# Up projection by seven products in slots, with operand splits ahead of their products, in the channel mixer of a decoder layer

## The chip, the cores and the metric

One Trainium2 chip, one core. The metric is the device time in microseconds (us) of one execution of the whole program. TensorE (PE) multiplies matrices into PSUM banks, VectorE (DVE), ScalarE (ACT) and GpSimd (POOL) work on tiles in SBUF, and SyncE (SP) issues all DMA transfers of this program on one queue.

## The reference

One layer over 2048 tokens, model width 1024, in float32. First a mixer (gated linear attention and an RWKV-7 group, chunk by chunk, with one input and one output projection), then the channel mixer, then a final norm:

```python
def conv_ffn(h, w_up, conv_w, conv_b, w_down):
    T = h.shape[1]
    u = h @ w_up
    up = jnp.pad(u, ((0, 0), (CONV_W - 1, 0), (0, 0)))
    u = sum(conv_w[j] * up[:, j:j + T] for j in range(CONV_W)) + conv_b
    gate, val = jnp.split(u, 2, axis=-1)
    return (jax.nn.silu(gate) * val) @ w_down
...
        mixed = jnp.concatenate([o_gla, o_rwkv], axis=-1) @ w_out[l]
        x = x + gt_m[:, None, :] * mixed
        h = modulate(x, norm_ffn_g[l], sh_f, sc_f)
        x = x + gt_f[:, None, :] * conv_ffn(h, ffn_up[l], ffn_conv_w[l], ffn_conv_b[l], ffn_down[l])
    return rms_norm(x, final_g)
```

The hidden width is 2816 = 22 x 128 for the gate and as much for the value.

## The kernel before

**Number format.** Every float32 operand of a large product is split into two parts, `hi` (a ScalarE cast, line 1138) and `lo` (the rest, a subtraction, line 1139), and each product is hi·hi + hi·lo + lo·hi: three matmuls of 128x512 for every 128 rows of the contraction. `split` takes VectorE or GpSimd for the subtraction by `either()` (line 1132): every third call is GpSimd's.

**First phase, to about 1431 us.** The mixer runs in 16 units over four blocks of 512 tokens. Its small matmuls leave gaps in TensorE's work; `fill()` (line 408) puts large matmuls of other work between them, `rate[0]` a step. In the last block `spare()` (line 1053), the output projection of blocks 0 to 2 (lines 276 to 278 and 445 to 447), is that filler, with `rate[0] = 0.8`, and `fill(100)` at the end issues what is left.

**Second phase, the channel mixer.** Two passes e = 0, 1 of two token blocks each (`stage_e`, line 1332). For each of 22 hidden tiles j the gate and the value of two blocks form a 2 x 2 problem that is done with seven products of half size and no eighth (a Strassen-Winograd scheme): `up_a` (line 1217) does M1 = a11·b11 and M2 = a12·b21, `up_b` (1234) M6, M7 and M5, and `up_c` (1247), a tile later, M3 and M4. The weight sums are GpSimd additions (lines 1224, 1225, 1226 and 1239). A product is 12 matmuls (lines 1212 to 1214). Banks are copied out by ScalarE (1228, 1238, 1244, 1251) and added by VectorE (1230, 1245, 1253). `conv` (1255) is the width-3 convolution: three small GpSimd copies for the halo (1257 to 1259), then per half an ACT activation and two VectorE operations (1263 to 1265). `hidden` (1269) is the gate: tanh, two VectorE operations, and the split of the result into `hh` and `hl` (1276 to 1281). Issue order per j: M1(j), M2(j), M3(j-1), M4(j-1), M6(j), M7(j), M5(j). When a group of hidden tiles is complete (2, then five times 4), `down_group` (line 1321) does its part of the down projection: 16 products of 3 matmuls per hidden tile (lines 1295 to 1297); each reads an accumulator tile `acc` from memory (1328), adds to it (1298) and writes it back (1330).

**Around it.** Before the first pass, `operands_a` and `operands_b` (1141, 1156) normalise the mixer's output and make the seven right-hand operands: I call this the entry. Between the passes (the transition) the output projection of block 3 (`stage_d`), the last down group and the operands of the second pass run together. After it the final norm (`finish`) ends the program.

**Who sets the order.** The program is written in the order above; a scheduler then sets each engine's order by priority (the place in the written order) and estimated times. Each engine, and SP's DMA queue, then works strictly in its order. Tiles come from rings: 8 for raw weights `w_st`, 4 for `w_hi`/`w_lo`, 6 for `ub`, 5 for `acc`, 6 PSUM banks. The tiles of the second phase lie where first-phase tiles lay, and one waits until what lay there is done with.

## Time and profile before

| | |
|---|---|
| median of 3 runs | 3055.96 us (3048.3 to 3060.26) |
| profiled execution, time / span | 3042.04 us / 3040.1 us |
| mean granted TensorE clock | 0.951 |
| busy share PE / DVE / ACT / POOL | 91% / 70% / 46% / 36% |
| DMA, mean over the span | 132 GB/s, hardware queue 42.0% of 16 engines |

The profile is of one execution. Times in it count from the start of its span. A row of the timeline gives the start, the duration, the engine, line and operation, and in brackets how long the engine was idle before it and what released it. A PE row's duration (0.39 us for a 128x512 matmul) overlaps its neighbours: the spacing of the starts is what a matmul costs. PEclk is the share of the full TensorE clock that was granted (1.00 is 2.4 GHz, 0.50 is 1.2 GHz).

### The profile page before, as it was taken

Reading aid. Unit: us, or ns where it says so; the run is one execution under the profiler, and the core shown is the slowest. Engines: PE = TensorE matmul, PEld = TensorE weight load, DVE = VectorE, ACT = ScalarE, POOL = GpSimd, SP = SyncE. Lnnn points to the kernel's source line nnn. Section 1 sums busy time; section 2 is a strip of 40 time slices with the busy share of each in tenths; the row PEclk is TensorE's granted clock in tenths of the full one; section 3 lists DMA queues with packets and bytes.
Section 4 is the critical chain, followed back from the end, with each engine's and each line's share of the span. In section 5 each row is a group of like instructions: output and inputs, shape, how many; then the busy total and the mean of one; then the engine's idle time right before and its main releaser. Section 6 shows DMA issues by size and latency. Waiting matters only on the chain. (4 is left out here: it accounts for less than half of the span.)

```text
span 3040.1 us, 54742 instructions
## 1 busy us (share of the span) xinstructions
PE 2776.1 (91%) x20296; PEld 2236.6 (74%) x20296; DVE 2136.3 (70%) x4248; ACT 1402.1 (46%) x2909; POOL 1102.1 (36%) x1193
## 2 busy tenths in 40 slices
PE   6998989999999999998599998989998998999997
PEld 5777777777787777777477777877776777877777
DVE  7368787877776778986877566574869756484766
ACT  4554445455554565554444334342544434342443
POOL 4223233323232224443534334252355424243441
PEclk9999998999999998999699999999998999999999
DMA  7555444443433344534142332424464442524332
GB/s 274 174 170 180 147 129 154 144 131 111 138 95 106 107 136 128 159 115 139 57 160 94 114 120 85 151 70 147 145 209 151 165 126 80 156 70 139 101 125 90
DMA packets 316875, 401.95 MB, mean 132 GB/s; under 512 B 75584, under 2 KB 148544, under 8 KB 316608
## 3 DMA queue, kind: packets, MB, share of 16 engines
q1 hardware_dynamic: 316608, 398.45, 42.0%
q8 instruction: 160, 2.62, 0.3%
q14 instruction: 107, 0.88, 0.1%
HBM read 293.49 MB, written 104.86 MB: 131 GB/s over the span
## 5 line engine op out<-in xcount | busy, mean ns | idle before, releaser
L1212 PE MATMUL g_bank<-h_hi,w_hi 128*128 128x512 f32 x1232 | 500.2, 408 | 66.9 <-ACT ub L1244 36.0
L1214 PE MATMUL g_bank<-h_hi,w_lo 128*128 128x512 f32 x1232 | 491.4, 404 | 46.4 <-POOL w_lo L1139 37.6
L1213 PE MATMUL g_bank<-h_lo,w_hi 128*128 128x512 f32 x1232 | 495.7, 402 | 7.5 <-DVE h_lo L1139 4.7
L1138 ACT CAST w_hi<-w_st 128x512 fp32r<-128x512 f32 (+1 forms) x396 | 241.0, 609 | 522.6 <-PE g_bank L1296 292.2
L1139 POOL TENSOR_TENSOR w_lo<-w_st,w_hi 128x512 fp32r<-128x512 f32 (+1 forms) x132 | 193.5, 1466 | 416.0 <-ACT w_hi L1138 376.0
L1212 PEld LDWEIGHTS g_bank<-h_hi,w_hi 128*128 128x128 f32 x1232 | 240.2, 195 | 132.3 <-ACT ub L1244 45.8
L1214 PEld LDWEIGHTS g_bank<-h_hi,w_lo 128*128 128x128 f32 x1232 | 239.8, 195 | 107.9 <-POOL w_lo L1139 41.7
L276 PE MATMUL g_bank<-h_hi,w_hi 128*128 128x512 f32 x736 | 297.5, 405 | 4.2 <-ACT carry L333 3.7
L1298 DVE SCALAR_TENSOR_TENSOR acc<-g_bank,mod,acc 128x512 f32<-128x512 f32 (+1 forms) x200 | 143.7, 727 | 217.8 <-PE g_bank L1297 179.9
L278 PE MATMUL g_bank<-h_hi,w_lo 128*128 128x512 f32 x736 | 296.0, 403 | 0.0
L277 PE MATMUL g_bank<-h_lo,w_hi 128*128 128x512 f32 x736 | 294.9, 401 | 0.0
L1213 PEld LDWEIGHTS g_bank<-h_lo,w_hi 128*128 128x128 f32 x1232 | 240.4, 195 | 62.1 <-DVE h_lo L1139 6.3
L1139 DVE TENSOR_TENSOR w_lo<-w_st,w_hi 128x512 fp32r<-128x512 f32 (+1 forms) x264 | 198.3, 752 | 83.3 <-ACT w_hi L1138 83.0
L1295 PE MATMUL g_bank<-hh,w_hi 128*128 128x512 f32 x640 | 247.2, 391 | 8.2 <-DVE acc L1298 5.3
L1296 PE MATMUL g_bank<-hl,w_hi 128*128 128x512 f32 x640 | 249.4, 392 | 1.2 <-DVE hl L1281 1.2
L1297 PE MATMUL g_bank<-hh,w_lo 128*128 128x512 f32 x640 | 247.5, 392 | 0.0
L179 ACT CAST w_hi<-w_st 128x512 fp32r<-128x512 f32 x272 | 167.5, 618 | 125.6 <-PE g_bank L277 75.5
L182 POOL TENSOR_TENSOR w_lo<-w_st,w_hi 128x512 fp32r<-128x512 f32 x90 | 125.8, 1398 | 265.4 <-ACT w_hi L179 215.8
L182 DVE TENSOR_TENSOR w_lo<-w_st,w_hi 128x512 fp32r<-128x512 f32 x182 | 139.9, 769 | 75.7 <-ACT w_hi L179 64.1
L276 PEld LDWEIGHTS g_bank<-h_hi,w_hi 128*128 128x128 f32 x736 | 140.5, 191 | 36.6 <-ACT carry L333 4.7
L278 PEld LDWEIGHTS g_bank<-h_hi,w_lo 128*128 128x128 f32 x736 | 140.9, 191 | 30.2 <-issue 0.2
L277 PEld LDWEIGHTS g_bank<-h_lo,w_hi 128*128 128x128 f32 x736 | 140.9, 191 | 28.6 <-issue 0.3
(348 smaller groups left out, 6248.9 us busy)
## 6 DMA issues: line engine op xcount, KB each, us to landing
acc<-acc SPq DMA_DIRECT2D x352, 256.0 KB, 3.1
w_st<-in_ffn_up SPq DMA_DIRECT2D x176, 256.0 KB, 2.7
w_st<-in_w_in SPq DMA_DIRECT2D x168, 256.0 KB, 3.0
proj<-ev SPq DMA_DIRECT2D x100, 256.0 KB, 3.0
w_st<-in_ffn_down SPq DMA_DIRECT2D x80, 256.0 KB, 2.7
w_st<-in_ada_t SPq DMA_DIRECT2D x64, 256.0 KB, 3.4
w_st<-in_w_out SPq DMA_DIRECT2D x64, 256.0 KB, 3.1
x_k<-in_x SPq DMA_DIRECT2D x48, 256.0 KB, 3.5
```

Of the source, the lines that this page charges most:

```text
L182: eng.tensor_tensor(out=lo[:, 0:w], in0=t[:, 0:w], in1=hi[:, 0:w].bitcast(F32), op=ALU.subtract)
L276: PE.matmul(out=ps, lhsT=wh, rhs=hi, start=k == 0, stop=False)
L277: PE.matmul(out=ps, lhsT=wh, rhs=lo, start=False, stop=False)
L278: PE.matmul(out=ps, lhsT=wl, rhs=hi, start=False, stop=k == KT - 1)
L1138: A.copy(out=hi, in_=t)
L1139: either().tensor_tensor(out=lo, in0=t, in1=hi.bitcast(F32), op=ALU.subtract)
L1212: PE.matmul(out=ps, lhsT=wh[:, c], rhs=hi, start=first and k == 0, stop=False, skip_group_check=True)
L1213: PE.matmul(out=ps, lhsT=wh[:, c], rhs=lo, start=False, stop=False, skip_group_check=True)
L1214: PE.matmul(out=ps, lhsT=wl[:, c], rhs=hi, start=False, stop=last and k == 3, skip_group_check=True)
L1295: PE.matmul(out=ps, lhsT=wh, rhs=hh, start=j == 0, stop=False)
L1296: PE.matmul(out=ps, lhsT=wh, rhs=hl, start=False, stop=False)
L1297: PE.matmul(out=ps, lhsT=wl, rhs=hh, start=False, stop=j == n - 1)
```

## The change

The up projection is written as a list of slots, one product each (`Up`, `Down`, `Other`), which `run` goes through: weights are loaded six slots ahead of their product (`load`, with the weight sums of M6), and split three slots ahead (`prep`). After each slot one piece of background work is written (`bg_step`): half a convolution, half a gate, one piece of the next operands, or, where there is none, a piece of the final norm. M3 and M4 of a tile now stand on both sides of M6 of the next, and a down group stands two products later: after M2 of the tile two behind its last one. In `parts_of` the `lo` subtraction alternates between VectorE and GpSimd for the up products and is VectorE's for all of `down`; over the program 22 of these subtractions move from VectorE to GpSimd. In the transition the output projection of block 3 is written ahead of the last down group, and the operands as background pieces. Rings: 9 `w_st` instead of 8; `ub` and the spread norms move to a pool of their own that is laid out last, the t1 operands too to one of their own; the scratch of the sums of squares shares the ring of `th`. Last, `rate[0]` in the mixer's last block is 0.55 instead of 0.8. The total number of instructions stays as it was. The core of the diff:

```diff
                 lag[0] = 2000
-                rate[0] = 0.8
+                rate[0] = 0.55
...
-    pools["np"], pools["nst"], pools["nhl"], pools["nev"], pools["nx"] = 2, 8, 4, 6, 5
+    pools["np"], pools["nst"], pools["nhl"], pools["nev"], pools["nx"] = 2, 9, 4, NX, NX
...
-        pl = h2p if name in ("b22", "t4") else h1p
+        pl = h2p if name in ("b22", "t4") else h0p if name == "t1" else h1p
...
-        return ap.tile([P, NB + 2], F32, name="ub", tag="ub", bufs=6)
+        return up.tile([P, NB + 2], F32, name="ub", tag="ub", bufs=6)
...
-    def parts_of(t, n=NB):
+    wturn = [0]
+    def parts_of(t, n=NB, down=False):
         pair = [pools["w"].tile([P, NB], F32R, name=f"w_{s_}", tag=f"w{s_}", bufs=pools["nhl"])[:, 0:n] for s_ in ("hi", "lo")]
-        split(t, pair)
+        wturn[0] += 1
+        split(t, pair, V if down or wturn[0] % 2 else G)
         return pair
...
+    bg, idle = [], []
+    def bg_step():
+        if bg:
+            bg.pop(0)()
+        elif idle:
+            idle.pop(0)()
...
+        def load(self):
+            u, j = self.u, self.j
+            half = lambda t, c: ffn_up[t][:, c * NB:(c + 1) * NB]
+            if self.what == 1:
+                u["a11"], u["a21"] = raw(half(j, 0)), raw(half(NH + j, 0))
+            elif self.what == 2:
+                u["a12"], u["a22"] = raw(half(j, 1)), raw(half(NH + j, 1))
+            elif self.what == 6:
+                u["s1"], u["s2"] = raw(), raw()
+                G.tensor_tensor(out=u["s1"], in0=u["a21"], in1=u["a22"], op=ALU.add)
+                G.tensor_tensor(out=u["s2"], in0=u["s1"], in1=u["a11"], op=ALU.add)
+                G.tensor_tensor(out=u["a21"], in0=u["a21"], in1=u["a11"], op=ALU.add)
+        def prep(self):
+            u = self.u
+            if self.what == 3:
+                G.tensor_tensor(out=u["s2"], in0=u["s2"], in1=u["a12"], op=ALU.add)
+            self.w = parts_of(u[{1: "a11", 2: "a12", 3: "s2", 4: "a22", 5: "s1", 6: "s2", 7: "a21"}[self.what]])
...
+        def post(self):
+            u, j = self.u, self.j
+            if self.what in (1, 3, 5, 6):
+                n_ = {1: "c11", 6: "c21", 5: "c22", 3: "c12"}[self.what]
+                u[n_] = ubt()
+                A.copy(out=u[n_][:, 2:NB + 2], in_=self.ps)
+            if self.what in (2, 4, 5):
+                n_ = {2: "c11", 4: "c21", 5: "c22"}[self.what]
+                o_ = u[n_][:, 2:NB + 2]
+                V.tensor_tensor(out=o_, in0=u["z"] if self.what == 5 else self.ps, in1=o_, op=ALU.add)
+            if self.what == 3:
+                u["cg"] = [None, None]
+                bg.extend(lambda i=i: conv(j, u, ("c11", "c12"), "cg", i) for i in range(2))
+            if self.what == 4:
+                u["cv"] = [None, None]
+                bg.extend(lambda i=i: conv(NH + j, u, ("c21", "c22"), "cv", i) for i in range(2))
+                bg.extend(lambda i=i: hidden(u, i, self.hid) for i in range(2))
...
+        def load(self):
+            k0, k1 = self.group
+            if self.i == 0:
+                self.shared["raw"] = raw(ffn_down[self.ft][:, k0 * P:k1 * P], (k1 - k0) * P)
+        def prep(self):
+            k0, k1 = self.group
+            if self.i == 0:
+                self.shared["w"] = parts_of(self.shared["raw"], (k1 - k0) * P, down=True)
+            self.a_ = acct()
+            nc.sync.dma_start(out=self.a_, in_=x2d[self.b][:, self.ft, :] if k0 == 0 else accd[self.b][self.ft])
...
+    def run(slots):
+        at, ahead_ = {"load": 0, "prep": 0}, {"load": 6, "prep": 3}
+        for s, slot in enumerate(slots):
+            for what in ("load", "prep"):
+                while at[what] < min(len(slots), s + ahead_[what] + 1):
+                    getattr(slots[at[what]], what)()
+                    at[what] += 1
+            slot.mm()
+            slot.post()
+            bg_step()
...
         for j in range(NH):
+            U(j, 1)
+            U(j, 2)
+            if j > 1 and group_of[j - 2] != group_of[j - 1]:
+                slots += down_slots(e, group_of[j - 2], hids[group_of[j - 2]])
+            if j > 0:
+                U(j - 1, 3)
+            U(j, 6)
+            if j > 0:
+                U(j - 1, 4)
+            U(j, 7)
+            U(j, 5)
...
+            def d_step(ft):
+                next(nxt["d"], None)
+                if ft == 0:
+                    nxt["h"], pieces = operands_a((e + 1) * HB)
+                    bg.extend(pieces)
+            def d_end():
+                for _ in nxt["d"]:
+                    pass
+                bg.extend(operands_b((e + 1) * HB + 1, nxt["h"]))
+            slots.append(Other(d_begin))
+            slots += [Other(lambda ft=ft: d_step(ft)) for ft in range(KT)]
+            slots.append(Other(d_end))
+            slots += down_slots(e, last, hids[last], sums)
```

The changed order stands in three places. First SP's queue at the end of a full down group of the first pass (hidden tiles 2 to 5; the next tile to be loaded is j = 8). Before; `w_st<-in_ffn_up` is a raw weight tile, `acc<-acc_...` an accumulator read, `acc_...<-acc` a write back:

```order
L1330 DMA acc_6_18108<-acc 128x512
L1328 DMA acc<-acc_0_18110 128x512
L1330 DMA acc_6_18116<-acc 128x512
L1199 DMA w_st<-in_ffn_up 128x512
L1328 DMA acc<-acc_1_18103 128x512
L1330 DMA acc_7_18109<-acc 128x512
L1328 DMA acc<-acc_1_18111 128x512
L1330 DMA acc_7_18117<-acc 128x512
L1199 DMA w_st<-in_ffn_up 128x512
L1328 DMA acc<-acc_2_18104 128x512
L1199 DMA w_st<-in_ffn_up 128x512 x9
```

Now (the last of the four loads of tile 8 is the one shown first):

```order
L1194 DMA w_st<-in_ffn_up 128x512
L1325 DMA acc<-acc_0_18108 128x512
L1333 DMA acc_6_18114<-acc 128x512
L1333 DMA acc_6_18122<-acc 128x512
L1325 DMA acc<-acc_0_18116 128x512
L1325 DMA acc<-acc_1_18109 128x512
L1333 DMA acc_7_18115<-acc 128x512
L1325 DMA acc<-acc_1_18117 128x512
L1333 DMA acc_7_18123<-acc 128x512
L1325 DMA acc<-acc_2_18110 128x512
L1194 DMA w_st<-in_ffn_up 128x512 x12
```

Two of the four loads of tile 8 stood behind accumulator reads of the next group, of which each needs a buffer that an earlier write back frees; now all four stand ahead of them.

Second, GpSimd just behind the same down group. Before; L1139 is first the split of M1(8), then that of M4(7):

```order
L1224 TENSOR_TENSOR w_st<-w_st 128x512
L1257 COPY ub<-ccar 128x2
L1259 COPY ccar<-ub 128x2
L1226 TENSOR_TENSOR w_st<-w_st 128x512
L1225 TENSOR_TENSOR w_st<-w_st 128x512
L1139 TENSOR_TENSOR w_lo<-w_st,w_hi 128x512
L1258 COPY ub<-ub 128x2
L1139 TENSOR_TENSOR w_lo<-w_st,w_hi 128x512
```

Now; L1125 is first the split of M4(6), then those of M5(7) and M2(8), and L1227 to L1229 are the sums of tile 8:

```order
L1125 TENSOR_TENSOR w_lo<-w_st,w_hi 128x512
L1227 TENSOR_TENSOR w_st<-w_st 128x512
L1229 TENSOR_TENSOR w_st<-w_st 128x512
L1228 TENSOR_TENSOR w_st<-w_st 128x512
L1275 COPY ub<-ccar 128x2
L1125 TENSOR_TENSOR w_lo<-w_st,w_hi 128x512
L1277 COPY ccar<-ub 128x2
L1125 TENSOR_TENSOR w_lo<-w_st,w_hi 128x512
```

What stood behind the first sum of tile 8 (the one that waits for its loads) was the split of the very next product, M1(8); now it is that of M5(7), three products on from the one that TensorE is then at.

Third, TensorE at the end of the mixer and the start of the entry. Before; L986 to L1020 are the last unit's state update, L232 and L245 the norm of the entry, L1212 to L1214 its first product M1(0):

```order
L232 MATMUL g_bank<-ones_121,x_ss 128x1 x4
L245 MATMUL g_bank<-ident,rn_120 128x128 x8
L986 MATMUL rs_bank<-rw_sv,rw_t 64x64 x8
L994 MATMUL rs_bank<-p1s,yf_655 64x64 x8
L1212 MATMUL g_bank<-h_hi,w_hi 128x512
L1213 MATMUL g_bank<-h_lo,w_hi 128x512
```

Now (L431 to L433 are the filler, L972 to L1006 the last state update, L219 and L232 the norm, L1249 the first product):

```order
L433 MATMUL g_bank<-h_hi,w_lo 128x512
L972 MATMUL rs_bank<-rw_sv,rw_t 64x64 x8
L980 MATMUL rs_bank<-p1s,yf_655 64x64 x8
L990 MATMUL rs_bank<-rw_uv,rw_bkt 64x64 x8
L219 MATMUL g_bank<-ones_121,x_ss 128x1 x4
L1006 MATMUL rs_bank<-rw_t,rw_sv 64x64 x8
L1010 MATMUL rs_bank<-rw_rbk,rw_uv 64x64 x8
L232 MATMUL g_bank<-ident,rn_120 128x128 x8
```

The last state update stood behind the norm and among the first product's matmuls; now it stands ahead of the spread of the norm, and 65 more filler matmuls (441 instead of 506 are issued by the second-last state update) stand between it and the update before.

## Rows read from the trace of the kernel before

**Rows 1.** Stretch, length; busy us (count) PE, PEld, DVE, ACT, POOL; PEclk; DMA share, GB/s.

```profile
1431.00:1515.00 84.00, 42.90 (x241) 30.47 (x242) 69.33 (x85) 36.34 (x64) 42.25 (x32) 0.67 0.30 97
...
1515.00:2260.00 745.00, 699.58 (x3006) 568.76 (x3005) 473.71 (x650) 304.61 (x509) 284.84 (x292) 0.97 0.40 127
2280.00:2356.00 76.00, 60.93 (x235) 46.78 (x234) 69.73 (x84) 37.51 (x64) 44.46 (x40) 0.86 0.46 150
2356.00:2960.00 604.00, 568.60 (x2419) 460.21 (x2418) 381.58 (x510) 238.02 (x400) 237.18 (x248) 0.97 0.38 119
2584.00:2660.00 76.00, 76.00 (x336) 62.76 (x335) 34.54 (x50) 23.54 (x38) 18.61 (x23) 1.00 0.50 156
```

**Rows 2.** Waits of PE, 1520 to 2270 us: total us, times, longest.

```profile
PE g_bank L1214 <- POOL w_lo L1139: 29.9, 4, 8.2
PE g_bank L1212 <- ACT ub L1244: 8.4, 9, 1.7
```

**Rows 3.** Waits of PE, 2380 to 2975 us.

```profile
PE g_bank L1212 <- ACT ub L1244: 27.6, 10, 5.3
PE g_bank L1214 <- POOL w_lo L1139: 4.7, 4, 2.6
```

**Rows 4.** Timeline of PE around the stall behind the group of tiles 2 to 5.

```profile
1720.67 0.79 PE L1214 MATMUL g_bank<-h_hi,w_lo 128*128 128x512 f32 x1 [7.40 <-POOL w_lo L1139]
1721.27 0.63 PE L1212 MATMUL g_bank<-h_hi,w_hi 128*128 128x512 f32 x1
...
1724.15 0.39 PE L1213 MATMUL g_bank<-h_lo,w_hi 128*128 128x512 f32 x1
```

**Rows 5.** Timeline of SP's queue ahead of that stall.

```profile
1708.45 0.32 SPq L1328 DMA_DIRECT2D acc<-acc  x1
...
1709.30 0.42 SPq L1199 DMA_DIRECT2D w_st<-in_ffn_up  x1
1711.99 0.32 SPq L1328 DMA_DIRECT2D acc<-acc  x1
1712.36 0.42 SPq L1199 DMA_DIRECT2D w_st<-in_ffn_up  x1
```

**Rows 6.** Timeline of POOL in and behind that stall.

```profile
1715.46 1.26 POOL L1224 TENSOR_TENSOR w_st<-w_st 128x512 f32<-128x512 f32 x1 [13.14 <-DMA w_st<-in_ffn_up]
...
1719.36 1.26 POOL L1139 TENSOR_TENSOR w_lo<-w_st,w_hi 128x512 fp32r<-128x512 f32 x1
...
1725.33 2.96 POOL L1139 TENSOR_TENSOR w_lo<-w_st,w_hi 128x512 fp32r<-128x512 f32 x1 [4.58 <-DVE cv L1265]
```

**Rows 7.** Timeline of DVE in and behind that stall.

```profile
1720.78 0.75 DVE L1264 SCALAR_TENSOR_TENSOR cv<-ub,ncw,cv 128x512 f32<-128x512 f32 x1 [10.29 <-POOL ub L1258]
...
1727.23 1.60 DVE L1277 SCALAR_TENSOR_TENSOR th<-th,cv 128x512 f32<-128x512 f32 x1
```

**Rows 8.** Timeline of ACT at the like stall in the second pass.

```profile
2533.76 0.62 ACT L1280 CAST hh<-th 128x512 fp32r<-128x512 f32 x1 [10.09 <-DVE th L1278]
...
2537.27 0.58 ACT L1244 COPY ub<-g_bank 128x512 f32<-128x512 f32 x1
```

**Rows 9.** Four lines' instructions, 1431 to 3040 us: ns min/median/max.

```profile
L1139 DVE TENSOR_TENSOR w_lo<-w_st,w_hi x264: 408/683/1787, 1447.3 to 2964.4; 128x512 fp32r<-128x512 f32 x128, 128x256 fp32r<-128x256 f32 x4
...
L1139 POOL TENSOR_TENSOR w_lo<-w_st,w_hi x132: 733/1295/3083, 1446.8 to 2958.0; 128x512 fp32r<-128x512 f32 x126, 128x256 fp32r<-128x256 f32 x6
L1225 POOL TENSOR_TENSOR w_st<-w_st x44: 1255/1290/1828, 1443.5 to 2936.5; 128x512 f32<-128x512 f32 x44
L1264 DVE SCALAR_TENSOR_TENSOR cv<-ub,vt,cv x88: 736/752/1835, 1506.5 to 2981.1; 128x512 f32<-128x512 f32 x88
L1258 POOL COPY ub<-ub x88: 176/581/2387, 1512.5 to 2983.3; 128x2 f32<-128x2 f32 x88
```

**Rows 10.** Busy time in two short stretches, columns as in Rows 1.

```profile
1488.00:1500.00 12.00, 2.81 (x4) 1.08 (x4) 11.30 (x12) 6.55 (x11) 7.17 (x5) 0.50 0.15 44
1520.00:1580.00 60.00, 57.11 (x249) 46.27 (x248) 41.96 (x63) 25.04 (x45) 17.76 (x24) 1.00 0.49 166
```

More of the change, by code (lines that the diff above doesn't have):

```diff
@@ L1134, in either, with piece @@
         return G if turn[0] % 3 == 0 else V
-    def split(t, pair):
-        hi, lo = pair
-        A.copy(out=hi, in_=t)
-        either().tensor_tensor(out=lo, in0=t, in1=hi.bitcast(F32), op=ALU.subtract)
     def operands_a(b):
-        rb = spread(ap, rn2[:, b])
+        rb = spread(up, rn2[:, b])
         hs = {"b11": [], "b21": []}
-        for k in range(KT):
-            pair = hc("b11" if k < 4 else "b21")
-            hs["b11" if k < 4 else "b21"].append(pair)
-            hi, lo = pair
+        def piece(k):
+            n_ = "b11" if k < 4 else "b21"
+            hi, lo = hc(n_)
+            hs[n_].append((hi, lo))
             xk = ubt()[:, 0:NB]
@@ L1164, in put @@
             hs[n_].append(pair)
-            split(t, pair)
+            split(t, pair, either())
         def whole(n_, k):
@@ L1171, in whole, with piece @@
             return d
-        for k in range(4):
+        def piece(k):
             two = []
@@ L1193, in operands_b @@
             put("t4", c)
-        return hs
+        return [lambda k=k: piece(k) for k in range(4)]
     def raw(src=None, n=NB):
@@ L1200, in raw @@
         return t
-    def parts_of(t, n=NB):
+    wturn = [0]
+    def parts_of(t, n=NB, down=False):
         pair = [pools["w"].tile([P, NB], F32R, name=f"w_{s_}", tag=f"w{s_}", bufs=pools["nhl"])[:, 0:n] for s_ in ("hi", "lo")]
-        split(t, pair)
-        return pair
-    def product(ps, t, ops, first, last):
-        wh, wl = parts_of(t)
-        for k in range(4):
-            c = slice(k * P, (k + 1) * P)
-            hi, lo = ops[k]
-            PE.matmul(out=ps, lhsT=wh[:, c], rhs=hi, start=first and k == 0, stop=False, skip_group_check=True)
-            PE.matmul(out=ps, lhsT=wh[:, c], rhs=lo, start=False, stop=False, skip_group_check=True)
-            PE.matmul(out=ps, lhsT=wl[:, c], rhs=hi, start=False, stop=last and k == 3, skip_group_check=True)
@@ new lines, in hidden @@
+    def hidden(u, i, hid):
+        cg, cv = u["cg"][i], u["cv"][i]
+        th = lp.tile([P, NB], F32, name="th", tag="th", bufs=2)
+        A.activation(out=th, in_=cg, func=AF.Tanh, scale=0.5)
+        V.scalar_tensor_tensor(out=th, in0=th, scalar=1.0, in1=cg, op0=ALU.add, op1=ALU.mult)
+        V.scalar_tensor_tensor(out=th, in0=th, scalar=0.5, in1=cv, op0=ALU.mult, op1=ALU.mult)
+        hh, hl = (lp.tile([P, NB], F32R, name="h" + s_, tag="h" + s_, bufs=4 * HB) for s_ in "hl")
+        A.copy(out=hh, in_=th)
+        V.tensor_tensor(out=hl, in0=th, in1=hh.bitcast(F32), op=ALU.subtract)
+        hid[i].append((hh, hl))
@@ L1318, in hybrid_kernel @@
[L1318 to L1330 removed]
+        return spread(up, r, ts)
@@ L1332, in stage_e, with finish_later, down_slots @@
+    def finish_later(b, sums):
+        rb = []
+        idle.append(lambda: rb.append(finish_head(b, sums)))
+        idle.extend(lambda ft=ft: finish_tile(b, ft, rb[0]) for ft in range(KT))
+    kgroups = ((0, 2), (2, 6), (6, 10), (10, 14), (14, 18), (18, 22))
+    def down_slots(e, g, hid, sums=None):
+        slots = []
+        for ft in range(KT):
+            shared = {}
+            slots += [Down(e * HB + i, i, ft, g, hid, shared, sums) for i in range(HB)]
+        return slots
     def stage_e(e, hs):
@@ L1333, in stage_e @@
         bs_ = range(e * HB, (e + 1) * HB)
+        hids = {g: [[], []] for g in kgroups}
         group_of = {j: g for g in kgroups for j in range(*g)}
[L1335 removed]
+        us = [{} for _ in range(NH)]
+        slots = []
+        U = lambda j, what: slots.append(Up(j, what, us[j], hs, hids[group_of[j]]))
         for j in range(NH):
[L1337 to L1351 removed]
@@ L1357, in stage_e @@
+        k0, k1 = last
         more = (e + 1) * HB < NBLK
@@ L1384, in stage_e @@
             pair = hc(next(wplace))
-            split(raw(ffn_down[ft][:, k0 * P:k1 * P]), pair)
+            split(raw(ffn_down[ft][:, k0 * P:k1 * P]), pair, V)
             ws.append(pair)
@@ L1394, in stage_e @@
             for ft in range(KT):
-                down(ft, ws[ft], hid, i, acc[i][ft], bs_[i], c)
+                down(ft, ws[ft], hids[last][i], acc[i][ft], c)
                 add_square(ap, sums[i][:, c], acc[i][ft][:, c], ft == 0, V)
-            at = tc.cur_priority
-            tc.cur_priority = at + LATE
-            finish(bs_[i], acc[i], sums[i], ts)
-            tc.cur_priority = at
-    hs = operands_b(1, operands_a(0))
+            rb = finish_head(bs_[i], sums[i], ts)
+            for ft in range(KT):
+                finish_tile(bs_[i], ft, rb, acc[i], c)
+    hs, pieces = operands_a(0)
+    for p_ in pieces:
+        p_()
+    for p_ in operands_b(1, hs):
+        p_()
     pools["norm"] = lambda: bank("rj")
```

241 lines of the change are left out of this document (96 added, 145 removed).

## Prediction, made before the changed kernel was run

> **What bounds the kernel now.** I read the stretches first, then the waits in them, then the timeline around the longest wait. At full speed the up projection runs 336 matmuls in 76 us, so 0.226 us each, with PE busy all the time (the stretch from 2584) [rows 1]. Against that price each stretch of the channel mixer loses: first pass 745 - 3006 x 0.226 = 66 us; second pass 604 - 2419 x 0.226 = 57 us; transition 76 - 235 x 0.226 = 23 us; entry, from PE's busy time, 84 - 42.9 = 41 us [rows 1]. Some matmul records may be missing, so these are upper values. TensorE bounds the channel mixer, then, but for about 187 us; the change can only get at those.
>
> In the two passes the waits named add up to 29.9 + 8.4 us and 27.6 + 4.7 us [rows 2, 3], 71 of the 123 us. The large ones come once per down group. The reader can follow one of them: SP holds two weight loads of the next tile behind accumulator reads that wait for a buffer, so they go out only at 1709.30 and 1712.36 [rows 5]; GpSimd's first sum waits 13.14 us for such a load, and the split of the next product stands behind the sums, at 1719.36 [rows 6]; TensorE waits 7.40 us for that split [rows 4]; VectorE's convolution waits 10.29 us for a halo copy on the same GpSimd queue [rows 7]. In the second pass the same late GpSimd holds the gate for 10.09 us on ScalarE, which works in order, and the bank copy behind it frees M3's bank at 2537.27, TensorE's 5.3 us there [rows 8, 3]. After each stall TensorE restarts at about half its rate (0.63 us a row instead of 0.39): nine matmuls from 1720.67 to 1724.15 take 3.48 us instead of 2.03 [rows 4], 1.4 us more, some 12 us over the eight stalls. About 83 us of the two passes are thus explained, and 40 are spread out, or missing records.
>
> In the entry VectorE is the bound: 11.30 us of 12 in one stretch, with PE at 2.81 us and the clock at 0.50 [rows 10]. In the transition it is busy 69.73 of 76 us [rows 1].
>
> **The change, part by part.**
>
> *Loads six slots ahead.* All loads of tile 8 now leave SP ahead of the accumulator reads of the next group, and those reads are written three slots ahead of their use. What stood behind GpSimd's waiting sum was the split of the next product; now it is one three products on. A slot is 12 x 0.226 = 2.7 us, so a sum may be late by some 8 us before TensorE notices, where it was 13.14 us late with almost no slack [rows 6]. I expect the large stall to go, with its slow restart: the four GpSimd stalls of the first pass and the long bank copies of the second. Late next are the gates of a group's last tile: they are written into the two slots before the group, and its first down product needs them after eight or nine of its matmuls, 2 us. The nearest row is the gate's wait of 10.09 us [rows 8], which is part of the stall; without a late GpSimd I take 1.5 us for each of ten groups, 15 us. Of 83 us explained I give back 70 (83 less 15, rounded, with 2 from smaller waits). Bounds: all 123 us if the unexplained part goes with them, 10 us if the wait of the gate takes most of the stall's place (ten groups at about 7 us).
>
> *Splits alternate; 22 go from VectorE to GpSimd.* Each costs 1.295 us there and saves 0.683 us on VectorE [rows 9]: 28 us more on an engine that is busy 285 of 745 us, 15 us less on the other. Nothing on the path, as long as GpSimd is ahead; what it costs without that cover is the second rival below.
>
> *Pieces of conv and gate instead of whole ones, bank copies ahead of the gate on ScalarE.* The same instructions; the copy that frees a bank no longer stands behind a cast that waits for VectorE. That is part of the 70 us, not counted again. The longer hold of three banks across a down group costs nothing while copies are early.
>
> *Transition.* The output projection of block 3 and the operand pieces are spread evenly and begin earlier. VectorE keeps its work there (69.73 us), so I give back half of 23 us: 11. Bounds 0 and 20.
>
> *Entry.* 65 filler matmuls, 65 x 0.226 = 15 us, move from inside the mixer to between its last two state updates, and the last state update goes ahead of the norm instead of through the entry. If the mixer was held by TensorE there, its chain ends up to 15 us sooner and the holes take the filler; if it was held by its own chain, the filler only comes later and TensorE's holes of the middle open, up to 15 us the other way. VectorE's work of the entry itself does not shrink, and it is the bound. I take +5, between -15 and +15. The other places of tiles could let the first operands begin sooner; no row shows them waiting for memory, so I count nothing.
>
> *Ninth weight buffer, the shared scratch ring, splits of the last group on VectorE, removed dead code:* nothing, each below 5 us by the busy time of its engine; the last stretch has no stall that they touch.
>
> *Sum:* 70 + 11 + 5 = 86 us. The profiled execution took 3042.04 us, 14 us less than the median of the runs, 3055.96. So 2956 us against the profiled one, and **2970 us** on the median's footing.
>
> **The rivals.**
>
> *The shared port (about 3030 us).* Where VectorE and GpSimd both work, their instructions lengthen: a split on GpSimd takes 2.96 us instead of 1.295, and beside it a VectorE operation 1.60 instead of about 0.7 [rows 6, 7, 9], as if only one of them ran at a time. If so, their durations alone add up. Per tile before: on VectorE 4.7 splits, 8 convolution operations at 0.752 and 6 of the gate, taken at the 0.683 of a split, 13.3 us; on GpSimd 2.3 splits and four sums at 1.29, 8.2 us [rows 9]; 21.5 us together. Now 3.5 and 3.5 splits: 22.2 us, while TensorE needs 84 x 0.226 = 19.0. Four tiles ask for 88.8 us in 76; about 7 us of that (three splits and the sums of the next tile) can be done during the down group, which asks little of either. So 6 us are left over per group, 60 us over ten, and the gain falls to 26. For it: the two long durations. Against it: in a stretch of 60 us VectorE and GpSimd are busy 41.96 + 17.76 us, so all of it, and TensorE still runs 249 x 0.226 = 56 us of work [rows 10]; work moves into the down groups more than I allow. The Trainium skill, "SBUF — State Buffer", section "Who interferes with whom", states the same as a rule: a VectorE instruction with two SBUF inputs and a GpSimd instruction that reads SBUF shut each other out for whole instructions. By that rule this change, which moves work to the slower of the two, comes out at the 3030 us of this rival; the two lengthened rows agree with it. Chance 0.16.
>
> *GpSimd becomes the bound of a tile (about 3230 us, slower).* Now 3.5 splits and 4 sums a tile are on GpSimd, and every second product waits for one. If each takes the 2.96 us of the one row, a tile takes 7.5 x 2.96 = 22.2 us, and its six halo copies 6 x 0.581 = 3.5 [rows 6, 9]: 25.7 instead of 19.0, so 6.7 x 44 = 295 us lost in place of 123, 172 us slower. It decides once the mean passes (19.0 + 123/44 - 3.5)/7.5 = 2.44 us. Against it: the median is 1.295 us [rows 9]. For it: the change makes GpSimd's splits regular, each beside VectorE work. Chance 0.11.
>
> *The stall moves and does not go (about 3050 us).* GpSimd's sum still waits for a load each tile, SP still holds loads behind write backs, and M5's split stands behind it; or the entry loses what the passes win. Chance 0.09.
>
> **How the numbers follow.** The forecast has 0.64. Its own range follows from the bounds of the passes (10 to 123), the transition (0 to 20) and the entry (-15 to 15), which will not all fall on one side: gains of 50 to 138 us, 2918 to 3006. To leave out no more than 2 in 10, the range goes to 3036 and takes in the port rival. A measurement of this kernel can tell some 0.5%, 15 us, from no change. Faster by more: the forecast and most of the port rival, 0.64 + 0.14 = 0.78. Within: the stall that moves and the rest, 0.11. Slower: 0.11.
>
> **What would show it.** Right: no wait of TensorE above 4 us behind a down group, sums of GpSimd that wait less than 5 us for their loads, a first pass below 700 us for its 3006 matmuls, and a mean clock above 0.951. Wrong: waits of `w_lo` from GpSimd at nearly every tile with durations near 2 us (the port), waits of the first down products for `hh` of several us (the gate is late next), or a stretch between the mixer and the first pass that is longer than 84 us. A total above 3036 us would mean that what the down groups lost was not lost to late loads at all.

## The result, and the profile after

The changed kernel takes 2954.67 us (median of 4 runs, 2950.25 to 2957.0), the kernel before 3058.11 (4 runs): a ratio of 0.9663, 95% interval 0.9635 to 0.9691, so 103 us faster. Forecast were 2970 us and a range of 2918 to 3036. The profiled execution took 2950.25 us, 91.8 less than the one profiled of before.

First busy time by stretch in the changed kernel, columns as in [rows 1]:

```profile
1431.00:1515.00 84.00, 50.35 (x300) 37.84 (x299) 66.61 (x87) 34.27 (x59) 45.81 (x32) 0.74 0.30 94
1585.00:2130.00 545.00, 541.38 (x2358) 441.05 (x2357) 401.07 (x490) 237.15 (x396) 268.42 (x250) 1.00 0.40 125
2225.00:2330.00 105.00, 86.87 (x351) 67.94 (x350) 88.89 (x109) 46.90 (x82) 64.60 (x51) 0.87 0.46 155
2350.00:2860.00 510.00, 507.46 (x2211) 413.75 (x2210) 369.25 (x451) 214.81 (x356) 243.25 (x230) 1.00 0.39 123
...
1707.20:1783.80 76.60, 76.46 (x338) 62.97 (x337) 68.38 (x81) 45.43 (x75) 47.89 (x48) 1.00 0.27 87
```

In both passes TensorE is now busy all but about 3 us, at the full clock throughout. The last row is the four tiles between two down groups: 338 matmuls in 76.60 us, 0.227 each, the price of full speed in [rows 1]. The losses that are left lie in the entry (the first row) and in the transition (the third). There TensorE's longest wait behind the mixer, 8.31 us, comes 15 us behind the last full down group of the first pass; before, no wait in the transition was longer than 3.3 us. GpSimd, VectorE and PE in it:

```profile
2238.72 1.71 POOL L1125 TENSOR_TENSOR w_lo<-w_st,w_hi 128x512 fp32r<-128x512 f32 x1
```

```profile
2239.23 1.75 DVE L1172 SCALAR_TENSOR_TENSOR ub<-ub,mod,rbc 128x512 f32<-128x512 f32 x1
```

```profile
2240.49 0.80 PE L1251 MATMUL g_bank<-h_hi,w_lo 128*128 128x512 f32 x1 [8.31 <-POOL w_lo L1125]
```

TensorE waits for a split that stands behind weight sums and operand work on GpSimd; from 2233 us GpSimd's instructions follow each other at 1.7 us each, and those of VectorE beside them take up to 1.77.

All of PE's waits, 1600 to 2130 us, to be held against [rows 2]:

```profile
PE g_bank L1251 <- POOL w_lo L1125: 1.5, 2, 1.0
PE g_bank L263 <- ACT w_hi L179: 1.1, 1, 1.1
PE g_bank L1249 <- ACT ub L1258: 0.8, 1, 0.8
```

and 2350 to 2860 us, against [rows 3]:

```profile
PE g_bank L1251 <- POOL w_lo L1125: 1.7, 4, 0.5
PE g_bank L1249 <- DVE acc L1309: 0.9, 1, 0.9
```

All lines of before for the windows of [rows 2, 3] make 77 us, 71 of them in the lines shown there; now it is 6 (in windows some 300 us shorter in all). The late load is not gone, though. GpSimd just behind a down group that ends at 1828.6 us, against [rows 6]:

```profile
1830.31 1.28 POOL L1227 TENSOR_TENSOR w_st<-w_st 128x512 f32<-128x512 f32 x1 [5.36 <-DMA w_st<-in_ffn_up]
1831.67 1.30 POOL L1229 TENSOR_TENSOR w_st<-w_st 128x512 f32<-128x512 f32 x1
1832.92 1.30 POOL L1228 TENSOR_TENSOR w_st<-w_st 128x512 f32<-128x512 f32 x1
1834.16 0.66 POOL L1275 COPY ub<-ccar 128x2 f32<-128x2 f32 x1
1834.77 1.29 POOL L1125 TENSOR_TENSOR w_lo<-w_st,w_hi 128x512 fp32r<-128x512 f32 x1
```

The first sum still waits 5.36 us for its load, and a split stands behind the three sums; but TensorE is at M3 of an older tile then, and its next splits are done. Of this wait GpSimd has 19.8 us in seven times between 1600 and 2130 us, where before it had 61.3 us in nine.

**Where the time went, stretch by stretch.** Both programs run the same number of 128x512 matmuls. I counted them from the end in PE's records and subtracted the times at which equally many were still to come; so each stretch below holds the same amount of work. The limits are the starts of the 5250th, 3150th, 2400th and 600th matmul from the last: 1651.34, 2177.92, 2399.62 and 2852.86 us in the execution before, 1655.58, 2141.11, 2354.22 and 2769.10 us in the one after; the last stretch goes to the end of the span. Each row is the difference of one profiled execution to the one before, in us; the runs e1 to e12 are described below.

| run | median us | mixer and entry | first pass | transition | second pass | end |
|---|---|---|---|---|---|---|
| changed kernel | 2954.67 | +4.2 | -41.0 | -8.6 | -38.4 | -7.9 |
| e1 | 3055.34 | +6.5 | +4.2 | +5.1 | -1.9 | +2.7 |
| e2 | 2962.80 | +18.2 | -40.6 | -7.3 | -39.8 | -8.2 |
| e3 | 3030.10 | +20.7 | -8.4 | -2.5 | -13.1 | -3.5 |
| e4 | 2941.81 | -3.7 | -41.2 | -8.6 | -39.1 | -8.0 |
| e5 | 2967.75 | +11.9 | -43.9 | +6.7 | -41.0 | -0.5 |
| e6 | 3000.32 | +20.2 | -24.9 | -2.6 | -25.0 | -7.1 |
| e7 | 2937.47 | -10.2 | -42.5 | -12.5 | -38.1 | -8.6 |
| e8 | 2958.17 | +10.0 | -39.7 | -9.3 | -37.9 | -8.3 |
| e9 | 3021.05 | +6.8 | -18.5 | +5.5 | -19.3 | +1.8 |
| e10 | 2954.87 | +9.8 | -39.9 | -7.2 | -38.6 | -7.9 |
| e11 | 2956.82 | +17.8 | -42.6 | -10.3 | -40.0 | -7.0 |
| e12 | 2965.35 | +20.1 | -39.4 | -11.3 | -39.1 | -8.1 |

The changed kernel's row sums to -91.7 us (the profiled times differ by 91.8). The two passes hold 79 of it. Limits elsewhere share it out otherwise. The stall at 2953.01 us before, a wait of 3.76 us for a bank copy, falls into the end, and a restart of the down group from 2182.82 us, behind waits for `hh` and `hl`, into the transition: limits 50 matmuls later would move 7 us from there to the first pass. With the ends of the prediction's own stretches in the execution before (1515, 2260, 2356 and 2960 us) and the same matmuls after, the first pass gained 48.0 us, the transition 12.7, the second pass 37.4 and the rest 2.5; ahead of 1515 us, 9.1 were lost.

### The profile page after: what moved, and what is told of

Its sections match the earlier page's. It is cut to its first block, busy times and chain, and to the rows that moved or that the text cites. A ratio compares the mean times of both kernels' runs of the same rounds, so it can differ in the third digit from the quotient of the medians.

```text
span 2948.5 us, 54765 instructions
## 1 busy us (share of the span) xinstructions
PE 2764.5 (94%) x20296; PEld 2231.9 (76%) x20296; DVE 2198.3 (75%) x4229; ACT 1407.2 (48%) x2909; POOL 1189.5 (40%) x1212
## 4 chain that ended last, share of the span: by engine, by line
PE 60%; DVE 15%; DMA 7%; issue 3%; ACT 2%; POOL 2%; SPq 0%; DVEq 0%; POOLq 0%; ACTq 0%
PE g_bank L1251 9%; PE g_bank L1249 9%; PE g_bank L1250 9%; PE g_bank L1306 5%; PE g_bank L1308 5%; PE g_bank L1307 5%; PE g_bank L263 3%; PE g_bank L265 3%; PE g_bank L264 3%; DMA w_st<-in_ada_t 1%; DVE w_lo L182 1%; PE gl_bank L679 1%; DMA x_k<-in_x 1%; DMA ub<-x 1%; DVE gl_d L652 1%
## 5 line engine op out<-in xcount | busy, mean ns | idle before, releaser
L1249 PE MATMUL g_bank<-h_hi,w_hi 128*128 128x512 f32 x1232 | 488.7, 397 | 29.0 <-ACT h_hi L1124 12.4
L1251 PE MATMUL g_bank<-h_hi,w_lo 128*128 128x512 f32 x1232 | 481.7, 396 | 16.8 <-POOL w_lo L1125 12.3
L1125 POOL TENSOR_TENSOR w_lo<-w_st,w_hi 128x512 fp32r<-128x512 f32 x154 | 221.5, 1439 | 229.2 <-ACT w_hi L1124 225.5
L263 PE MATMUL g_bank<-h_hi,w_hi 128*128 128x512 f32 x736 | 299.3, 408 | 5.2 <-ACT carry L320 3.8
L265 PE MATMUL g_bank<-h_hi,w_lo 128*128 128x512 f32 x736 | 297.4, 405 | 3.5 <-DVE w_lo L182 3.5
L1249 PEld LDWEIGHTS g_bank<-h_hi,w_hi 128*128 128x128 f32 x1232 | 235.5, 191 | 84.3 <-ACT h_hi L1124 14.7
L1251 PEld LDWEIGHTS g_bank<-h_hi,w_lo 128*128 128x128 f32 x1232 | 235.7, 191 | 71.6 <-POOL w_lo L1125 17.8
L182 POOL TENSOR_TENSOR w_lo<-w_st,w_hi 128x512 fp32r<-128x512 f32 x90 | 128.3, 1425 | 228.6 <-ACT w_hi L179 191.5
L1125 DVE TENSOR_TENSOR w_lo<-w_st,w_hi 128x512 fp32r<-128x512 f32 (+1 forms) x242 | 201.1, 831 | 19.4 <-ACT w_hi L1124 19.4
```

The costliest lines, as they stand in the source:

```text
L182: eng.tensor_tensor(out=lo[:, 0:w], in0=t[:, 0:w], in1=hi[:, 0:w].bitcast(F32), op=ALU.subtract)
L263: PE.matmul(out=ps, lhsT=wh, rhs=hi, start=k == 0, stop=False)
L265: PE.matmul(out=ps, lhsT=wl, rhs=hi, start=False, stop=k == KT - 1)
L1125: eng.tensor_tensor(out=lo, in0=t, in1=hi.bitcast(F32), op=ALU.subtract)
L1249: PE.matmul(out=ps, lhsT=wh[:, c], rhs=hi, start=first and k == 0, stop=False, skip_group_check=True)
L1251: PE.matmul(out=ps, lhsT=wl[:, c], rhs=hi, start=False, stop=last and k == 3, skip_group_check=True)
```

## The experiments

**e1: loads ahead of the down group, in the kernel before.**

```diff
             if ready is not None:
+                up_load(j + 1)
                 down_group(e, *ready, hid.pop(ready))
```

> The kernel before, with one thing added: the four weight loads of the next hidden tile are written ahead of a down group instead of behind it. Theory A (the stall behind each down group comes from weight loads that stand behind accumulator reads on SP's queue): TensorE's waits for GpSimd's w_lo in the first pass fall from 29.9 us to under 8, the long waits for the bank copy L1244 in the second pass from 27.6 to under 14, and the time falls by 40 to 75 us, to about 3000. Rival B (it is the splits three slots ahead that cover everything; a load earlier only moves the wait to the next instruction of GpSimd's queue): within 15 us of the kernel before, 3043 to 3073, with the waits still there under other names.

3055.34 us, ratio 0.9994 (0.998 to 1.0009): no difference. SP's queue and then GpSimd behind the group of tiles 2 to 5 in this run:

```profile
1716.30 0.38 SPq L1337 DMA_DIRECT2D acc<-acc  x1
1716.74 0.42 SPq L1199 DMA_DIRECT2D w_st<-in_ffn_up  x1
1719.38 0.32 SPq L1335 DMA_DIRECT2D acc<-acc  x1
1719.75 8.54 SPq L1199 DMA_DIRECT2D w_st<-in_ffn_up  x2
```

```profile
1722.78 1.26 POOL L1231 TENSOR_TENSOR w_st<-w_st 128x512 f32<-128x512 f32 x1 [14.00 <-DMA w_st<-in_ffn_up]
```

The edit did not do what it says: loads still stand between accumulator reads, one goes out only at 1719.75 us, and the sum waits 14.00 us until it has landed. SP's waits from 1690 to 1730 us (L1335 is the accumulator read, L1199 the weight load):

```profile
SPq L1335 <- DMA acc<-acc: 22.1, 8, 4.4
SPq L1199 <- POOL ub L1265: 7.8, 1, 7.8
...
SPq L1199 <- DVE cv L1272: 0.3, 1, 0.3
SPq L1199 <- DVE w_lo L1139: 0.2, 1, 0.2
```

The 7.8 us belong to the load behind the one at 1719.75 us. Up to that one the weight loads themselves wait 0.5 us in all; it is the accumulator reads ahead of them on the queue that wait, for earlier transfers of accumulators. So when the program ran, the order on the queue held the load back, and not a weight buffer. Why the scheduler kept that order, the run doesn't show. It speaks neither for theory A nor against it, since the loads did not move.

**e2: splits written one slot ahead.** In `run`, with the accumulator reads kept at three:

```diff
-        at, ahead_ = {"load": 0, "prep": 0}, {"load": 6, "prep": 3}
+        at, ahead_ = {"load": 0, "prep": 0, "read": 0}, {"load": 6, "prep": 1, "read": 3}
...
```

> The changed kernel with the splits one slot ahead of their product instead of three (accumulator reads stay three ahead, loads six). Theory A (loads are what mattered): a split takes some 2 us of its 2.7 us slot, so small waits appear at many products, 10 to 35 us in all: 2965 to 2990. Rival B (the three slots of lead give the gain): the passes lose most of their 82 us again, 3015 to 3050, with waits of TensorE for w_lo at nearly every product.

2962.80 us, ratio 0.9674 (0.9644 to 0.9705). PE's waits in 2400 to 2850 us are one line:

```profile
PE g_bank L1254 <- POOL w_lo L1125: 0.4, 1, 0.4
```

The passes gain 40.6 and 39.8 us, as with three slots: neither the loss of rival B nor the 10 to 35 us of small waits of theory A came. But the splits did not move. From 1600 to 2100 us, with the first split that ends set against the first product that needs one and so on, 5.2 us lie at the median between a split's end and the first matmul with its result, 5.3 in the changed kernel and 6.7 in the one before. So what a later split would cost is not shown; against rival B speaks that the splits of the kernel before were no later at the median. The 8 us in the median are in the mixer and entry (+18.2 in the table), of which more below.

**e3: the old order of products and place of the down group, in the changed kernel.**

```diff
+            if j > 0:
+                U(j - 1, 3)
+                U(j - 1, 4)
             U(j, 6)
             U(j, 7)
             U(j, 5)
+            if j > 0 and group_of[j - 1] != group_of[j]:
+                slots += down_slots(e, group_of[j - 1], hids[group_of[j - 1]])
```

> The changed kernel with the products in the old order: M1, M2, M3 and M4 of the tile before, M6, M7, M5, and the down group right behind M5, two products earlier than now. Loads and splits keep their leads of six and three slots. Theory A: loads are still ahead of the accumulator reads for the most part, so the passes lose little, 2955 to 2980. Rival C (the place of the down group and M6 between M3 and M4 give gates and banks the time they need): first down products of every group wait for hh, 3 us or more at ten groups, and M6 waits for its bank: 2990 or more.

3030.10 us, ratio 0.9902 (0.9874 to 0.993). The passes keep only 21 of their 79 us. Behind a group, GpSimd and ScalarE:

```profile
1732.84 1.29 POOL L1227 TENSOR_TENSOR w_st<-w_st 128x512 f32<-128x512 f32 x1 [8.56 <-DMA w_st<-in_ffn_up]
```

```profile
1743.39 0.62 ACT L1292 CAST hh<-th 128x512 fp32r<-128x512 f32 x1 [8.24 <-DVE th L1290]
...
1746.90 1.07 ACT L1258 COPY ub<-g_bank 128x512 f32<-128x512 f32 x2
```

The time is that of rival C, but the rows show the chain of before: a late load, a sum that waits 8.56 us for it, the gate's cast that waits behind, and a bank copy that lets TensorE go on after 4.49 us. First down products did not wait for `hh`, as rival C had it. So the order decides, and by way of the late load.

**e5 and e6: no late loads, in the old order.** Sums take the loaded gate half for the value half. In the kernel before:

```diff
-        a11, a12, a21, a22 = (raw(w_[:, c * NB:(c + 1) * NB]) for w_ in (gw, vw) for c in range(2))
+        a11, a12 = (raw(gw[:, c * NB:(c + 1) * NB]) for c in range(2))
+        a21, a22 = raw(), a12
...
-        G.tensor_tensor(out=s1, in0=a21, in1=a22, op=ALU.add)
+        G.tensor_tensor(out=s1, in0=a11, in1=a22, op=ALU.add)
...
```

> The kernel before with the value half of the up weights never loaded: the sums take the gate half in its place, so each tile has two weight loads instead of four and GpSimd's sums wait for no load that M1 and M2 do not need too; products, sums, splits and their order in the code stay. Left out: the value half of the up projection. The first run meant to bring loads forward did not do so (its loads still went out late and GpSimd's sum still waited 14.00 us), so it decided nothing. Theory A (late loads, by way of GpSimd's sums, make the stall behind each down group): the 29.9 us of waits for w_lo fall under 8, the bank copy's 27.6 us under 14, time 2975 to 3020. Rival C (it is the old order of products and the place of the down group that stall, whatever the loads do): the stalls stay, 3040 to 3065.

2967.75 us, ratio 0.9707 (0.9681 to 0.9734). PE's waits, 1520 to 2230 and 2350 to 2900 us, first lines:

```profile
PE g_bank L1212 <- ACT ub L1245: 4.6, 4, 1.5
PE g_bank L1212 <- ACT ub L1239: 3.7, 2, 3.5
...
PE g_bank L1212 <- ACT ub L1245: 2.8, 2, 2.0
```

Late loads have become few: GpSimd's first sum waits for one 3 times, 22.1 us in all, from 1520 to 2130 us, where before it did 10 times, 69.5 us. TensorE's wait for GpSimd's split is gone [rows 2], the bank copy's 27.6 us are 2.8 [rows 3], and the passes gain 43.9 and 41.0 us: a little more than the changed kernel's, without its order, leads, pieces or buffers. This is more than theory A asked for. Half of the up loads are missing from the queue and a tile needs a buffer fewer, so it shows what late weight loads cost, not by itself which of queue and buffers makes them late.

The same in e3's kernel:

> The kernel of the third run (changed kernel, old order of products and old place of the down group) with the value half of the up weights not loaded, as in the run beside it; left out: the value half of the up projection. Theory A: the order matters only because it sets how soon behind a down group a fresh tile's loads are due, so without late loads the old order costs little: 2945 to 2985. Rival C: the old order stalls by itself, 3010 to 3035.

3000.32 us, ratio 0.9814 (0.9795 to 0.9832): between both. The passes gain 50 us where e3 had 21. The largest wait that is left is for the copy of a bank, in 1520 to 2230 us:

```profile
PE g_bank L1249 <- ACT ub L1258: 12.8, 8, 2.2
```

It comes once between two groups, 47 us behind the end of one (at 1764.45 us 2.17, at 2016.32 us again 2.17), not right behind it. So the slot program in the old order also has a smaller loss of its own, 29 us over the passes against the changed kernel. The kernel before does not have it without late loads (e5). Why is open.

**e9: the new order alone, in the kernel before.** `up_c` is cut in two, and a group runs after M2 of the next tile but one:

```diff
             u = up_a(j, hs)
+            if ready is not None:
+                down_group(e, *ready, hid.pop(ready))
+                ready = None
             if prev is not None:
                 up_c(prev[1], hs)
-            up_b(u, hs)
+            up_b(u, hs, mid)
...
```

> The kernel before with the new order alone: M1, M2, then the down group of the tile two behind, M3 of the tile before, M6, M4, M7, M5. No slots, no leads, no pieces; splits, buffers and filler rate as before. If the order by itself keeps late loads from what TensorE needs next (a tile's four loads precede the group, the next tile's are due five products behind it): the passes gain 50 to 80 us, 2975 to 3010. If the leads and pieces of the slot program are needed with it: less than 25 us, 3030 to 3060.

3021.05 us, ratio 0.9885 (0.9851 to 0.9919): between the two cases again. The passes gain 38 us, half of the 79. The stall behind the groups has gone: the longest wait for GpSimd's split is 2.5 us. In its place the down groups wait. PE in 2350 to 2900 us, then ScalarE in one group:

```profile
PE g_bank L1299 <- DVE acc L1302: 20.3, 12, 3.0
```

```profile
2604.46 0.62 ACT L1138 CAST w_hi<-w_st 128x512 fp32r<-128x512 f32 x1 [3.38 <-DMA w_st<-in_ffn_down]
2611.63 0.62 ACT L1138 CAST w_hi<-w_st 128x512 fp32r<-128x512 f32 x1 [6.55 <-DMA w_st<-in_ffn_down]
```

It is a late load once more, now of down weights: the cast waits 6.55 us, VectorE's split behind it, the accumulation behind that on VectorE, and TensorE for the bank that it would free. A full group takes 47 to 50 us instead of the 44.6 of the changed kernel. The loads of this run are in fact later: in four full groups of the first pass a down weight goes out 12.0 us ahead of its first matmul at the median, in the changed kernel 23.6 and in the one before 29.5; the last up load 9.4 us ahead of M1 instead of 13.7.

**e10: loads written three slots ahead.**

```diff
-        at, ahead_ = {"load": 0, "prep": 0}, {"load": 6, "prep": 3}
+        at, ahead_ = {"load": 0, "prep": 0}, {"load": 3, "prep": 3}
```

> The changed kernel with loads (and M6's sums) three slots ahead instead of six. If the lead of six is part of the gain, as the prediction had it: sums wait for loads again and the passes lose 20 to 60 us, 2975 to 3015. If the order alone does it: within 12 us of the changed kernel, 2945 to 2967.

2954.87 us, ratio 0.9662 (0.9637 to 0.9688), the changed kernel's time. Here too nothing moved: of tiles 3 to 21 of the first pass, the last load goes out 12.3 to 17.8 us ahead of M1 (median 13.7, five slots), in the changed kernel 11.7 to 17.2 (median 13.7). The written lead of six is no part of the gain, then; what a lead that is really shorter would cost, the run doesn't show.

**e11: splits shared as before.**

```diff
-        split(t, pair, V if down or wturn[0] % 2 else G)
+        split(t, pair, G if wturn[0] % 3 == 0 else V)
```

> The changed kernel with every third weight split on GpSimd again, those of the down projection too, instead of every second one of the up products. Shared port rival: fewer splits on the slower engine take 0.7 us a tile off the two engines together, so it is faster by 10 to 30 us, 2925 to 2945. If TensorE is covered either way: within 12 us, 2945 to 2967.

2956.82 us, ratio 0.9664 (0.9633 to 0.9695), no difference. Where the 22 splits run does not matter here, and the price that the shared port rival put on them falls. Its premise was seen: two lengthened rows [rows 6, 7], as the Trainium skill has it ("SBUF — State Buffer", section "Who interferes with whom"), and that rule speaks against a share of every second split for GpSimd. But in the stretch of 76.60 us above, where VectorE and GpSimd are busy 68.38 + 47.89 us, TensorE ran at full speed all the while: what the two lose to each other is covered here. Nor did they take turns all through it: with each instruction at the shortest that its kind takes anywhere behind 1431 us, their work in that stretch would still be 56.7 + 34.6 = 91.3 us. In the transition it is not covered. Around 2240 us both work without a pause, VectorE's instructions take up to 1.77 us instead of about 0.7 and GpSimd's 1.7 instead of 1.3, and TensorE waits 8.31 us, as shown above. That agrees with the rule, and there the port is a cost that the kernel still pays; in e11 TensorE waits 7.1 us at the like place, for a split on VectorE. How much of these waits the lengthening alone makes was not tried.

**e4, e8, e7 and e12: the mixer's end and the entry.** e4 and e8 change only the rate of filler in the mixer's last block:

```diff
-                rate[0] = 0.55
+                rate[0] = 0.8
```

> The changed kernel with the old rate of filler in the mixer's last block, 0.8 instead of 0.55. By the count of large matmuls, the end of the mixer and the entry together are some 4 us slower in the changed kernel than in the one before, though 5 us faster was forecast. Theory D (the deferred filler only comes later and the mixer's chain does not end sooner): 0.8 gives these 4 to 10 us back, 2944 to 2951. Rival E (the deferral helps, and the entry is slower for another reason, such as its order or the places of its tiles): 0.8 makes it 5 to 20 us slower, 2960 to 2975.

> The changed kernel with filler rate 1.0. Theory D (filler put off only comes later): another 2 to 8 us less than at 0.8, 2934 to 2940. Rival (the filler runs out before the last unit, whose chain then leaves TensorE idle): 2943 to 2955.

e4 takes 2941.81 us, ratio 0.9618 (0.9594 to 0.9642), and its slowest run (2944.77) is below the changed kernel's fastest; e8 at rate 1.0 takes 2958.17, ratio 0.9673 (0.9645 to 0.9702). e7 adds to 0.8 two products of tile 1 ahead of M6(0), with that tile's value half loaded later:

```diff
+            if j == 0:
+                U(1, 1)
+                U(1, 2)
...
```

> The changed kernel with the filler rate 0.8, and at the start of each pass M1 and M2 of tile 1 written ahead of M6 of tile 0, so that TensorE has 24 matmuls more that need only the operands b11 and b21 while VectorE makes the others. If TensorE's holes of the entry can be filled this way: 4 to 12 us less than with the rate alone (2941.81), 2930 to 2938. If VectorE bounds the entry so closely that two more splits there put off the operands by as much: 2940 to 2948.

> The seventh run (M1 and M2 of tile 1 early) with filler rate 0.7 instead of 0.8. The mixer and the entry were 13 us faster at 0.8 than at 0.55 and 16 us slower at 1.0 than at 0.8. If the optimum is near 0.8: 2937 to 2947. If it lies between 0.55 and 0.8: 2925 to 2936.

e7 takes 2937.47 us (2929.98 to 2942.02), ratio 0.9607 (0.9585 to 0.9629), the fastest of all; its step of 4 us over e4 is within what runs differ by. e12, the same at 0.7, takes 2965.35, ratio 0.9693 (0.9666 to 0.9719). What the early products do show is in the transition: the wait of 8.31 us is gone in both runs that have them (none above 3.7 us there), and their rows are 3.9 and 2.7 us better than those of the changed kernel and e4. With 0.55, 0.7, 0.8 and 1.0 at 2955, 2965, 2942 and 2958 us (the second with e7's edit), the rate has no simple effect: e4 came out on theory D's side, e8 against it, and rival E fell with e4. I can say only that the changed kernel's 0.55 is not its best value, and that 0.8 is better by 13 us.

## Why the prediction was right, and where it was not

**What bounds the kernel: right.** The 79 us that the passes gain are about [rows 2, 3] and the slow restarts: the 71 us of named waits and 12 of restarts were nearly the whole of what could be had. (The stretch of 3.48 us in the prediction is eight spacings, not nine, so a restart costs 1.7 us and not 1.4.) Of the 40 us "spread out, or missing records", none is missing records: the traces hold all 22 x 2 x 7 x 12 = 3696 up matmuls. Some 14 us of them are the price of the down matmuls, 44.57 us for a full group of 192, so 0.233 each instead of 0.226, over about 2000 in both passes. That late loads are the root is shown by e5, with the limit named there.

**The term "loads six slots ahead", 70 us: the size was near, the part named was not.** The passes gave 79 us, and 85 by the prediction's own stretches. But six slots written instead of three bring nothing (e10), and three for splits nothing over one (e2): neither edit moved what it names, so the written leads are not what gains, and real ones were not tested. Of its two reasons the second one holds, that "what stood behind GpSimd's waiting sum was the split of the next product; now it is one three products on"; and what makes it so is the order of products: M1 and M2 of a tile now come before the group, so its four loads must too, and the next tile's are due five products behind it. I had written that order down as part of the change and given it no term. Undone alone, it takes back 58 of the 79 us (e3); made alone, it brings 38 (e9), because late loads then show up in the down groups. What lets the changed kernel's down weights go out 23.6 us ahead and not 12.0 (the ninth buffer, accumulator reads three ahead, all down splits on VectorE, or the slots themselves) was not tried apart.

**The gate late next, 15 us held back: did not come.** No wait of a down product for `hh` is among those of either pass. By size that is the difference between 70 and 85.

**Splits to GpSimd at nothing, conv and gate in pieces at nothing of their own:** the first is shown by e11; the second was not tried. That GpSimd becomes the bound of a tile did not happen either: its split took 1.296 us in the median and 1.439 in the mean after the change,

```profile
L1125 POOL TENSOR_TENSOR w_lo<-w_st,w_hi x154: 1263/1296/2863, 1448.9 to 2877.5; 128x512 fp32r<-128x512 f32 x154
```

```profile
L1125 POOL TENSOR_TENSOR w_lo<-w_st,w_hi 128x512 fp32r<-128x512 f32 x154 | 221.5, 1439 | 229.2 <-ACT w_hi L1124 225.5
```

far from the mean of 2.44 us at which that rival decides. The port rival's sum left out three additions of banks a tile on VectorE (four tiles kept it busy 68.38 us, 17 each, where the sum has 12.5 a tile), and TensorE was covered even so. The rival of the stall that moves was half right: the late load stayed, and the stall did not.

**Transition, 11 us: right,** as far as it can be told: 8.6 by the table, 12.7 by the prediction's own stretches, both within the bounds of 0 and 20. That VectorE keeps its work there held, and a new stall of 8.31 us came with it.

**Entry, +5: the wrong way.** Of the prediction's two cases the second came. The mixer's state update (L1020 before, L1006 now) comes in groups of 16 matmuls; the third group from the end is issued by 1409.2 us instead of 1413.7, so the chain is 4.5 us ahead there. But 101 filler matmuls stand behind it instead of 36, and 65 x 0.226 = 15 us are more than that. The first product, M1(0), starts at 1454.61 us instead of 1443.90, 10.7 later. From there to the first limit of the table the entry is 6.4 us shorter (201.0 instead of 207.4), with VectorE busy 66.61 of 84 us at its start where it was 69.33. One execution could mislead here (below), but six with 0.55 start M1(0) at 1454.6 to 1469.1 us and four of the old code at 1443.9 to 1457.5, and e4 gains 13 us by the old rate alone.

**The end, nothing: nearly so.** Behind 2960 us it gave 2.5 us, most of it at a wait of 1.95 us for `hh` before, at 2988.27 us. The other 5 us of that column are the stall at 2953.01 us, which is one of [rows 3].

**The footing.** 86 us were forecast and 91.8 came between profiled executions; 103 between medians, since the execution profiled before was 16 us below the median of the four runs (14 below that of the three known then) and the one after 4 below. That the sum came so close is in part luck: by the prediction's own stretches the passes gave 15 us more than forecast and the entry some 14 less.

Of the signs named, the clock (0.960 against 0.951) and the first pass (its stretch of 745 us takes 697 for the same matmuls) came out as for the forecast, and so did the waits inside the passes. Two did not: 15 us behind the last full down group of the first pass TensorE waits 8.31 us, not under 4, and the sums wait 5.4 us at the longest, not below 5.

## What to carry to other kernels

A late transfer costs by what stands behind its waiting instruction on the same engine and by how soon that is needed: put the products whose operands are already there right behind the stretch that delays loads, and the load may stay late. Written leads count for little where a scheduler sets the order on the queue: three edits here (e1, e2, e10) moved nothing. Read the issue times in the trace before you believe an edit has moved them, and before you call a run a test. And try the order alone before building leads, pieces and buffers around it, then look for where the same wait comes up next.

## What the runs showed that I had not expected

The same written mixer takes different times from execution to execution. Its last state update, as four executions have it whose code up to there is the same (changed kernel, e2, e10, e11):

```profile
L1006 PE MATMUL rs_bank<-rw_t,rw_sv x512: 218/218/366, 341.6 to 1447.0; 64*64 64x64 f32 x171
```

```profile
L1006 PE MATMUL rs_bank<-rw_t,rw_sv x512: 218/218/366, 342.5 to 1460.9; 64*64 64x64 f32 x171
```

```profile
L1006 PE MATMUL rs_bank<-rw_t,rw_sv x512: 218/218/366, 344.4 to 1455.8; 64*64 64x64 f32 x171
```

```profile
L1006 PE MATMUL rs_bank<-rw_t,rw_sv x512: 218/218/366, 345.4 to 1458.6; 64*64 64x64 f32 x171
```

It starts last at 1447.0 to 1460.9 us, a spread of 14 us, while each of their passes agrees within 3 us. The runs of e2 alone reach from 2948.56 to 2965.22 us. A term of a few microseconds in the mixer can't be read from one profile, and the column "mixer and entry" of the table has to be read with that.
